# Gate and up projections run together, with a seven-product scheme on three of eight row pairs

## The chip, the cores and the metric

The kernel runs on one core of one Trainium2 chip. The core has a matrix engine (TensorE, in the profile PE for its matmuls and PEld for its weight loads), a vector engine (VectorE, DVE), an activation engine (ScalarE, ACT), GpSimd (POOL) and a queue engine (SyncE, SP) that here only issues DMAs. Matmul results land in PSUM, which has eight banks of 128 x 512 fp32; everything else lives in SBUF. The metric is the device time of one execution in microseconds, the median of several runs.

## What is computed

One hybrid decoder layer on 256 tokens of width 2048: a norm and an input projection, then attention and a state-space mixer side by side, an output projection with a residual, a SwiGLU feed-forward of inner width 5632, and a gated per-layer embedding. The change lies in the feed-forward:

```python
hf = rms_norm(x, g_ffn_norm[i])
x = x + (jax.nn.silu(hf @ w_gate[i]) * (hf @ w_up[i])) @ w_down[i]
```

`hf` is 256 x 2048, `w_gate` and `w_up` are 2048 x 5632, `w_down` is 5632 x 2048, all fp32.

## The kernel before

**Arithmetic.** Each fp32 operand is split into a high part (`hi`, type fp32r, made by an ACT copy) and a low part (`lo`, the fp32 value minus `hi`, made by a VectorE subtraction). A product is three matmuls, `hi*hi + hi*lo + lo*hi`, added up in one PSUM bank.

**Weights.** `Weights` cuts every weight matrix into chunks of 2 x 128 rows by up to 512 columns, in the order in which they are used. `load_to` issues a chunk's DMA on SP into one of `RAW = 5` raw buffers, `split_to` makes its high and low part in one of `PART = 3` buffers each, and `take(i)` asks for the splits up to chunk i+2 and the loads up to chunk i+7. The splits are written inside `high_priority(W_AHEAD)` with `W_AHEAD = 70`.

**Order of the instructions.** The program is written as one stream. A planner then orders each engine's queue: among the instructions that are ready it takes the one with the lowest rank, which is the place at which it was written, less 70 inside `high_priority(W_AHEAD)`, plus 25 for `gate_task` and plus 100 for `norm_task` (table `AHEAD`). Instructions inside such a block don't advance the rank of what follows. `Sched` runs small tasks (Python generators such as `norm_task` and `gate_task`) between the matmuls of a chunk. `S` hands out 39 SBUF slots of 4 KB per partition, `PP` four PSUM banks; the other four banks are the accumulators `acc`.

**Gate and up** (lines 1313 to 1346). For each of 11 blocks of 512 columns, `block` runs all 16 row tiles (k-tiles) of `w_gate`, then all 16 of `w_up`. Each run uses two accumulators, one per half of the tokens (t = 0, 1), so that a block alternates between two pairs of banks:

```python
for b in range(11):
    acc = block(blk["gu"][b][0], lhs_f, need_f if b == 0 else None)
    ...
        act(wsg[b % 2][:, t], acc[t], AF.Silu, scale=r_f[:, t:t + 1])
    acc = block(blk["gu"][b][1], lhs_f)
    for t in range(2):
        tt(wsg[b % 2][:, t], acc[t], wsg[b % 2][:, t])
    sched.add(gate_task(b), 0)
```

In `chunk` the last chunk of a run finishes token half 0 before half 1. `gate_task` transposes the gated block through a `PP` bank and splits it into `gh` and `gl`. `fh` and `fl` are the split, normed activations; `norm_task` makes them while the output projection runs, also through `PP` banks.

**Down** (lines 1349 to 1367) runs 44 row tiles for each of four column blocks, reading `gh` and `gl`. The parts of the per-layer embedding's input (`prh`, `prl`) are written behind its first block.

Of the kernel before, what the change touches and what calls it, by code (L numbers as in the profile page):

```python
# [11 lines left out]
F32 = mybir.dt.float32  # L12
# [129 lines left out]
class Weights:  # L142
# [4 lines left out]
    def __init__(self, tc, pool, sched):  # L147
        self.tc, nc = tc, tc.nc
        self.nc, self.pool, self.sched, self.chunks = nc, pool, sched, []
        self.raw, self.part, self.n_dma, self.n_split = {}, {}, 0, 0  # L150
        self.extra, self.native = {}, set()

    def block(self, w, k0, nk, c0, n):
        ids = []
# [21 lines left out]
    def split_to(self, i):  # L176
        while self.n_split <= min(i, len(self.chunks) - 1):
            self.load_to(self.n_split)
            n = self.chunks[self.n_split][3]
            raw = self.raw.pop(self.n_split)  # L180
            if self.n_split in self.native:
                self.part[self.n_split] = (raw, None, 0.0)
                self.n_split += 1
                continue
            hi = self.pool.tile([128, 2, n], F32R, tag="w_hi", bufs=self.PART, name="w_hi")
            lo = self.pool.tile([128, 2, n], F32R, tag="w_lo", bufs=self.PART, name="w_lo")
            with self.tc.high_priority(W_AHEAD):
                self.nc.scalar.activation(out=hi, in_=raw, func=AF.Copy)  # L188
                self.nc.vector.tensor_tensor(out=lo, in0=raw, in1=hi.bitcast(F32), op=ALU.subtract)  # L189
            s = self.sched  # L190
            s.act += 2 * n * 0.83e-3 + 0.19
            s.dve = max(s.dve + 2 * n * 1.05e-3 + 0.06, s.act)
            self.part[self.n_split] = (hi, lo, s.dve)
            self.n_split += 1

    def take(self, i):
        self.split_to(i + self.PART - 1)
# [7 lines left out]
def hybrid_layer_kernel(  # L205
# [35 lines left out]
    blk["glu"] = [W.block(w_glu, 0, 8, 512 * b, 512) for b in range(2)]  # L241
    blk["wos"] = [W.block(w_o, 8, 8, 512 * b, 512) for b in range(4)]
    blk["gu"] = []
    for b in range(11):
        blk["gu"].append((W.block(w_gate, 0, 16, 512 * b, 512), W.block(w_up, 0, 16, 512 * b, 512)))
    blk["down"] = [W.block(w_down, 0, 44, 512 * b, 512) for b in range(4)]
    blk["pp"] = [W.block(w_ple_proj, 0, 2, 512 * b, 512) for b in range(4)]
    blk["ple"] = [W.block(w_ple_gate, 0, 16, 512 * b, 512) for b in range(4)]
# [779 lines left out]
            sched.flags.add("oa")  # L1028


    def norm_task(xt, cb, ss, hi, lo, g0, flag):

        for t in range(2):
            pt = yield from pp_get("n")
            act(pt, xt(t, cb), AF.Square, accum_out=ss[:, cb, t:t + 1])
            PP.put(pt)
        for i0 in range(0, 4, 2):
            pt = yield from pp_get("n")
            for i in range(2):
                for t in range(2):  # L1040
                    transpose(quarter(pt, 2 * i + t), xt(t, cb)[:, (i0 + i) * 128:(i0 + i) * 128 + 128])
            yield None
            yield from splits(*((hi[cb][:, i0 + i], lo[cb][:, i0 + i], pt[:, i * 256:i * 256 + 256],
                                 gc[:, g0 + 4 * cb + i0 + i:g0 + 4 * cb + i0 + i + 1]) for i in range(2)))
            PP.put(pt)
        sched.flags.add(f"{flag}{cb}")
        yield 1
# [249 lines left out]

    fh = wait_n(4, [128, 4, 256], "fh", F32R)
    fl = wait_n(4, [128, 4, 256], "fl", F32R)
    lhs_s = tiles4(sh, sl, 8)  # L1300

    def need_s(k):
# [2 lines left out]
    for b in range(4):  # L1305
        acc = block(blk["wos"][b], lhs_s, need_s)
        sched.until("os")
        residual(acc, r_s, b)
        sched.add(norm_task(xv, b, ss_f, fh, fl, G_FFN, "hf"), 0)
    S.put(*sh, *sl)  # L1310


    lhs_f = tiles4(fh, fl)
    wsg = wait_n(2, [128, 2, 512], "wsg")
    gh, gl = [], []

    def gate_task(b):
        h = yield from S.get([128, 4, 256], "gh", F32R)
        l = yield from S.get([128, 4, 256], "gl", F32R)
        gh.append(h)  # L1320
        gl.append(l)
        f2 = lambda a: a.rearrange("p k n -> p (k n)")
        for i0 in range(0, 4, 2):
            pt = yield from pp_get("g")
            for i in range(2):
                for t in range(2):
                    transpose(quarter(pt, 2 * i + t), wsg[b % 2][:, t, (i0 + i) * 128:(i0 + i) * 128 + 128])
            yield None
            yield from splits((f2(h[:, i0:i0 + 2]), f2(l[:, i0:i0 + 2]), pt, None))
            PP.put(pt)  # L1330
        sched.flags.add(f"g{b}")

    def need_f(k):
        sched.until(f"hf{(k + 1) // 4}")

    for b in range(11):
        acc = block(blk["gu"][b][0], lhs_f, need_f if b == 0 else None)
        if b == 0:
            total_rstd(r_f, ss_f)
        for t in range(2):  # L1340
            act(wsg[b % 2][:, t], acc[t], AF.Silu, scale=r_f[:, t:t + 1])
        acc = block(blk["gu"][b][1], lhs_f)
        for t in range(2):
            tt(wsg[b % 2][:, t], acc[t], wsg[b % 2][:, t])
        sched.add(gate_task(b), 0)
    S.put(*fh, *fl)
    lhs_g = tiles4(gh, gl)

    def need_g(k):
        sched.until(f"g{k // 4}")  # L1350

    ph, pl = [], []
    for b in range(4):
# [122 lines left out]
```

## Time and profile before

| what | value |
| --- | --- |
| median of 3 runs | 1156.77 us (1155.93 to 1158.2) |
| the profiled execution: its time, its span | 1154.46 us, 1152.4 us |
| granted TensorE clock, mean | 0.999 |
| stretch of gate and up (316.1 to 804.6) | 488.5 us |
| stretch of down (804.6 to 1047.4) | 242.8 us |

The profile is one execution. Its span runs from the first to the last instruction; the execution's own time is 2.06 us longer. Rows give an engine, an operation, the tiles it writes and reads, a count, busy time and the mean of one in ns; "idle before" is the time in which the engine stood still just ahead of the group's instructions, with what ended it. Matmuls are pipelined: the time from one to the next is shorter than the duration shown.

### The profile page before, as it was taken

The numbers are of one execution on the slowest core, as the hardware profiler recorded it, in microseconds if no ns is written. First come the engines' busy times: TensorE is split into PE (matmuls) and PEld (weight loads), VectorE is DVE, ScalarE is ACT, GpSimd is POOL, SyncE is SP. The second block draws the span as 40 slices with busy tenths as digits, with TensorE's granted clock in tenths as the row PEclk, the third lists the DMA queues.
The fourth block names the chain that finished last, engine by engine and source line by source line (L and its number), as shares of the span: only waits on it lengthen the run. The fifth ranks groups of instructions, "written<-read, shape, count | busy, mean of one in ns | idle before, by whom it ended". The sixth has DMA issues, their size and how long they took to land.

```text
span 1152.4 us, 15432 instructions
## 1 busy us (share of the span) xinstructions
PE 1133.4 (98%) x5938; PEld 943.3 (82%) x5938; DVE 678.1 (59%) x949; ACT 573.7 (50%) x815; POOL 19.0 (2%) x40
## 2 busy tenths in 40 slices
PE   9998999999999999999999999999999999999998
PEld 6877877898888888888888888888888888888886
DVE  7989998657755455455454454455445454545554
ACT  7864984546554444444444444444444343436443
POOL 1000020000000000000000000000000000000000
PEclk9999999999999999999999999999999999999999
DMA  9996371355566666666666666666556556565662
GB/s 333 242 266 193 115 230 37 112 192 178 178 193 189 194 185 198 185 186 196 185 190 192 186 192 190 187 193 189 190 192 188 193 186 197 184 199 184 207 213 91
DMA packets 112185, 216.95 MB, mean 188 GB/s; under 512 B 8032, under 2 KB 12912, under 8 KB 112112
## 3 DMA queue, kind: packets, MB, share of 16 engines
q1 hardware_dynamic: 109808, 211.23, 60.5%
q0 software_dynamic: 2304, 4.74, 1.4%
q8 instruction: 46, 0.75, 0.3%
q14 instruction: 27, 0.22, 0.1%
HBM read 212.66 MB, written 3.28 MB: 187 GB/s over the span
## 4 chain that ended last, share of the span: by engine, by line
PE 88%; DVE 6%; ACT 2%; DMA 2%; issue 2%; POOL 0%; DVEq 0%; SPq 0%; ACTq 0%; POOLq 0%
PE acc L319 82%; DVE w_lo L189 1%; DMA e<-in_bE_dram 1%; PE pp_g L346 1%; PE pp_at L319 1%; DVE w L710 1%; PE pp_at L963 1%; PE pp_n L346 1%; PE pp_v L691 1%; ACT L315 1%; PE pp_y L745 1%; DVE w L303 1%; DVE wp L303 0%; ACT w_hi L188 0%; DMA rope<-in_ivf_dram 0%
## 5 line engine op out<-in xcount | busy, mean ns | idle before, releaser
L189 DVE TENSOR_TENSOR w_lo<-w_raw,w_hi 128x1024 fp32r<-128x1024 f32 (+2 forms) x382 | 462.3, 1211 | 435.4 <-ACT w_hi L188 435.0
L188 ACT ACTIVATE w_hi<-w_raw 128x1024 fp32r<-128x1024 f32 (+2 forms) x382 | 400.7, 1049 | 531.5 <-PE acc L319 520.0
L319 PE MATMUL acc<-w_hi,fh 128*128 128x512 f32 x704 | 274.9, 390 | 0.0
L319 PE MATMUL acc<-w_hi,fl 128*128 128x512 f32 x704 | 274.8, 390 | 0.0
L319 PE MATMUL acc<-w_lo,fh 128*128 128x512 f32 x704 | 274.0, 389 | 0.0
L319 PEld LDWEIGHTS acc<-w_hi,fl 128*128 128x128 f32 x704 | 132.2, 188 | 28.0
L319 PEld LDWEIGHTS acc<-w_lo,fh 128*128 128x128 f32 x704 | 132.2, 188 | 27.2
L319 PEld LDWEIGHTS acc<-w_hi,fh 128*128 128x128 f32 x704 | 132.2, 188 | 26.9
L319 PE MATMUL acc<-w_hi,gh 128*128 128x512 f32 x352 | 137.3, 390 | 0.0
L319 PE MATMUL acc<-w_hi,gl 128*128 128x512 f32 x352 | 137.1, 389 | 0.0
L319 PE MATMUL acc<-w_lo,gh 128*128 128x512 f32 x352 | 137.0, 389 | 0.0
L319 PEld LDWEIGHTS acc<-w_hi,gl 128*128 128x128 f32 x352 | 66.1, 188 | 13.9
L319 PEld LDWEIGHTS acc<-w_lo,gh 128*128 128x128 f32 x352 | 66.1, 188 | 13.6
L319 PEld LDWEIGHTS acc<-w_hi,gh 128*128 128x128 f32 x352 | 66.1, 188 | 13.4
L319 PE MATMUL acc<-w_hi,ph 128*128 128x512 f32 x128 | 49.8, 389 | 0.0
L319 PE MATMUL acc<-w_lo,ph 128*128 128x512 f32 x128 | 49.8, 389 | 0.0
L319 PE MATMUL acc<-w_hi,pl 128*128 128x512 f32 x128 | 49.8, 389 | 0.0
L319 PE MATMUL acc<-w_lo,hh 128*128 128x512 f32 (+1 forms) x120 | 45.2, 376 | 2.4 <-DVE w_lo L189 2.3
L319 PE MATMUL acc<-w_hi,hl 128*128 128x512 f32 (+1 forms) x120 | 44.3, 371 | 0.0
L319 PE MATMUL acc<-w_hi,hh 128*128 128x512 f32 (+1 forms) x120 | 44.3, 376 | 0.0
L319 PE MATMUL acc<-w_hi,o 128*128 128x512 f32 x128 | 41.6, 399 | 0.1
L319 PEld LDWEIGHTS acc<-w_lo,hh 128*128 128x128 f32 x120 | 22.5, 188 | 7.6 <-DVE w_lo L189 4.3
(275 smaller groups left out, 1181.7 us busy)
## 6 DMA issues: line engine op xcount, KB each, us to landing
w_raw<-in_w_gate_dram SPq DMA_DIRECT2D x88, 512.0 KB, 3.6
w_raw<-in_w_up_dram SPq DMA_DIRECT2D x88, 512.0 KB, 3.7
w_raw<-in_w_down_dram SPq DMA_DIRECT2D x88, 512.0 KB, 3.6
w_raw<-in_w_o_dram SPq DMA_DIRECT2D x32, 512.0 KB, 3.7
w_raw<-in_w_ple_gate_dram SPq DMA_DIRECT2D x32, 512.0 KB, 4.3
w_raw<-in_w_in_dram SPq DMA_DIRECT2D x24, 512.0 KB, 7.9
w_raw<-in_w_glu_dram SPq DMA_DIRECT2D x8, 512.0 KB, 3.6
w_raw<-in_w_uq_dram SPq DMA_DIRECT2D x8, 384.0 KB, 4.4
```

What stands on the lines that cost most here:

```text
L188: self.nc.scalar.activation(out=hi, in_=raw, func=AF.Copy)
L189: self.nc.vector.tensor_tensor(out=lo, in0=raw, in1=hi.bitcast(F32), op=ALU.subtract)
L303: V.tensor_tensor(out=o, in0=a, in1=b, op=op)
L315: A.activation(out=o, in_=i, func=f, **k)
L319: T.matmul(out=o, lhsT=a, rhs=b, start=start, stop=stop)
L346: T.transpose(out=o, in_=i, identity=ident if idt is None else idt)
L691: T.matmul(out=pv[p, r * 256 + i4 * 64:r * 256 + i4 * 64 + 64], lhsT=ee[r][p, i * 64:i * 64 + 64], rhs=um[p, i, :], start=True, stop=True, ...
L710: V.tensor_tensor_scan(out=w, data0=dc, data1=w, initial=0.0, op0=ALU.mult, op1=ALU.add)
L745: T.matmul(out=o, lhsT=a[p, i, :], rhs=f[p, i, :], start=False, stop=(r == 1), tile_position=(64 * s, 64 * s))
L963: T.matmul(out=o, lhsT=a, rhs=b_, start=False, stop=(i == 1), skip_group_check=True)
```

## The change

Row tiles are taken in eight pairs, and gate and up of a pair run together. With A the 2 x 2 block matrix of activations (token half by row tile of the pair) and W the 2 x 2 block matrix of weights (row tile of the pair by gate or up), a pair is a 2 x 2 block product. A plain pair computes its eight tile products. A mixed pair (pairs 2, 4 and 6; in block 0 only 4 and 6) uses the Winograd form of Strassen's scheme, with seven.

- `mix` makes, for a mixed pair, the five weight operands that the seven products need besides the gate chunk itself: four additions of 512 columns, and high and low parts of five 512-column tiles. It writes one set of tiles, `w_last`, `w_sum` and `w_mix`, used by every mixed pair in turn. The up chunk of a mixed pair is not split otherwise.
- `row_sums`, called from `norm_task`, makes the four sums of activation tiles for pairs 2, 4 and 6, once.
- `mixed_block` runs a block with all four accumulators. The four products that enter more than one result (P1, P5, P6, P7) collect over the mixed pairs of the block in the four `PP` banks; `shared` combines them in SBUF behind the last mixed pair, and the end of the block adds the accumulators.
- `gate_task` now only transposes and copies the gated block (`gr`); `need_g` splits it into `gh` and `gl` in the down stage, and frees its slot.

```diff
--- before.py
+++ after.py
@@ -149,6 +149,7 @@
         self.nc, self.pool, self.sched, self.chunks = nc, pool, sched, []
         self.raw, self.part, self.n_dma, self.n_split = {}, {}, 0, 0
         self.extra, self.native = {}, set()
+        self.mixed, self.kept, self.sums = set(), {}, None
 
     def block(self, w, k0, nk, c0, n):
         ids = []
@@ -178,6 +179,12 @@
             self.load_to(self.n_split)
             n = self.chunks[self.n_split][3]
             raw = self.raw.pop(self.n_split)
+            if self.n_split in self.mixed:
+                self.part[self.n_split] = self.mix(self.kept.pop(self.n_split - 1), raw)
+                self.n_split += 1
+                continue
+            if self.n_split + 1 in self.mixed:
+                self.kept[self.n_split] = raw
             if self.n_split in self.native:
                 self.part[self.n_split] = (raw, None, 0.0)
                 self.n_split += 1
@@ -192,6 +199,33 @@
             s.dve = max(s.dve + 2 * n * 1.05e-3 + 0.06, s.act)
             self.part[self.n_split] = (hi, lo, s.dve)
             self.n_split += 1
+
+    def mix(self, g, u):
+
+
+        V, A, s = self.nc.vector, self.nc.scalar, self.sched
+        last, raws, parts = self.sums
+
+        def add(o, a, b):
+            V.tensor_tensor(out=o, in0=a, in1=b, op=ALU.add)
+
+        def part(h, l, r):
+            A.activation(out=h, in_=r, func=AF.Copy)
+            V.tensor_tensor(out=l, in0=r, in1=h.bitcast(F32), op=ALU.subtract)
+
+        with self.tc.high_priority(W_AHEAD):
+            add(raws[0][:, 0], g[:, 0], u[:, 0])
+            add(raws[0][:, 1], u[:, 0], u[:, 1])
+            part(last[:, 0], last[:, 1], u[:, 1])
+            add(raws[1][:, 0], raws[0][:, 0], u[:, 1])
+            add(raws[1][:, 1], raws[1][:, 0], g[:, 1])
+            for r, (h, l) in zip(raws, parts):
+                part(h, l, r)
+        s.act += 5 * 512 * 0.83e-3 + 3 * 0.19
+        s.dve = max(s.dve + 9 * 512 * 1.05e-3 + 0.42, s.act)
+        (h0, l0), (h1, l1) = parts
+        return ((last[:, 0], last[:, 1]), (h0[:, 0], l0[:, 0]), (h0[:, 1], l0[:, 1]),
+                (h1[:, 0], l1[:, 0]), (h1[:, 1], l1[:, 1])), None, s.dve
 
     def take(self, i):
         self.split_to(i + self.PART - 1)
@@ -241,8 +275,14 @@
     blk["glu"] = [W.block(w_glu, 0, 8, 512 * b, 512) for b in range(2)]
     blk["wos"] = [W.block(w_o, 8, 8, 512 * b, 512) for b in range(4)]
     blk["gu"] = []
+    MIXED = (2, 4, 6)
     for b in range(11):
-        blk["gu"].append((W.block(w_gate, 0, 16, 512 * b, 512), W.block(w_up, 0, 16, 512 * b, 512)))
+        ids = []
+        for j in range(8):
+            ids.append((j, W.block(w_gate, 2 * j, 2, 512 * b, 512)[0], W.block(w_up, 2 * j, 2, 512 * b, 512)[0]))
+            if j in (MIXED[1:] if b == 0 else MIXED):
+                W.mixed.add(ids[-1][2])
+        blk["gu"].append(ids)
     blk["down"] = [W.block(w_down, 0, 44, 512 * b, 512) for b in range(4)]
     blk["pp"] = [W.block(w_ple_proj, 0, 2, 512 * b, 512) for b in range(4)]
     blk["ple"] = [W.block(w_ple_gate, 0, 16, 512 * b, 512) for b in range(4)]
@@ -1028,7 +1068,19 @@
             sched.flags.add("oa")
 
 
-    def norm_task(xt, cb, ss, hi, lo, g0, flag):
+    def row_sums(o, r):
+
+        tmp, hi, lo = o
+        a11, a21, a12, a22 = (r[:, 128 * i:128 * i + 128] for i in range(4))
+        s = [tmp[:, 128 * i:128 * i + 128] for i in range(4)]
+        tt(s[0], a22, a21, ALU.subtract)
+        tt(s[2], a11, a21, ALU.subtract)
+        tt(s[1], a11, s[0], ALU.add)
+        tt(s[3], a12, s[1], ALU.subtract)
+        act(hi, tmp, AF.Copy)
+        tt(lo, tmp, hi.bitcast(F32), ALU.subtract)
+
+    def norm_task(xt, cb, ss, hi, lo, g0, flag, mixed=None):
 
         for t in range(2):
             pt = yield from pp_get("n")
@@ -1042,6 +1094,15 @@
             yield None
             yield from splits(*((hi[cb][:, i0 + i], lo[cb][:, i0 + i], pt[:, i * 256:i * 256 + 256],
                                  gc[:, g0 + 4 * cb + i0 + i:g0 + 4 * cb + i0 + i + 1]) for i in range(2)))
+            if mixed is not None and 2 * cb + i0 // 2 in mixed:
+                k, o = 4 * cb + i0, mixed[2 * cb + i0 // 2]
+                w = yield from S.get([128, 2, 512], "rows")
+                for i in range(2):
+                    act(w[:, 0, 256 * i:256 * i + 256], pt[:, i * 256:i * 256 + 256], AF.Copy,
+                        scale=gc[:, g0 + k + i:g0 + k + i + 1])
+                yield None
+                row_sums((w[:, 1], o[:, 0], o[:, 1]), w[:, 0])
+                S.put(w)
             PP.put(pt)
         sched.flags.add(f"{flag}{cb}")
         yield 1
@@ -1297,6 +1358,7 @@
 
     fh = wait_n(4, [128, 4, 256], "fh", F32R)
     fl = wait_n(4, [128, 4, 256], "fl", F32R)
+    rows = {j: wait_get([128, 2, 512], "sum", F32R) for j in MIXED}
     lhs_s = tiles4(sh, sl, 8)
 
     def need_s(k):
@@ -1306,19 +1368,20 @@
         acc = block(blk["wos"][b], lhs_s, need_s)
         sched.until("os")
         residual(acc, r_s, b)
-        sched.add(norm_task(xv, b, ss_f, fh, fl, G_FFN, "hf"), 0)
+        sched.add(norm_task(xv, b, ss_f, fh, fl, G_FFN, "hf", rows), 0)
     S.put(*sh, *sl)
 
 
     lhs_f = tiles4(fh, fl)
     wsg = wait_n(2, [128, 2, 512], "wsg")
-    gh, gl = [], []
+    uc = wait_get([128, 2, 512], "uc")
+    W.sums = (wait_get([128, 2, 512], "w_last", F32R), wait_n(2, [128, 2, 512], "w_sum"),
+              [wait_n(2, [128, 2, 512], "w_mix", F32R) for _ in range(2)])
+    gr, gh, gl = [], [], []
 
     def gate_task(b):
-        h = yield from S.get([128, 4, 256], "gh", F32R)
-        l = yield from S.get([128, 4, 256], "gl", F32R)
-        gh.append(h)
-        gl.append(l)
+        h = yield from S.get([128, 4, 256], "g")
+        gr.append(h)
         f2 = lambda a: a.rearrange("p k n -> p (k n)")
         for i0 in range(0, 4, 2):
             pt = yield from pp_get("g")
@@ -1326,28 +1389,111 @@
                 for t in range(2):
                     transpose(quarter(pt, 2 * i + t), wsg[b % 2][:, t, (i0 + i) * 128:(i0 + i) * 128 + 128])
             yield None
-            yield from splits((f2(h[:, i0:i0 + 2]), f2(l[:, i0:i0 + 2]), pt, None))
+            act(f2(h[:, i0:i0 + 2]), pt, AF.Copy)
             PP.put(pt)
         sched.flags.add(f"g{b}")
-
-    def need_f(k):
-        sched.until(f"hf{(k + 1) // 4}")
+        yield 1
+
+    def products(o, a, w, first, last):
+        mm(o, a[0], w[0], first, False)
+        mm(o, a[0], w[1], False, False)
+        mm(o, a[1], w[0], False, last)
+        sched.pe += 3 * 0.227
+
+    def pair(j, cg, cu, acc, pq, lhs, rows, first, last):
+
+
+        k = W.chunks[cg][1]
+        wh, wl = W.take(cg)
+        G = [(wh[:, i], wl[:, i]) for i in range(2)]
+        if pq is None:
+            for c, cid in enumerate((cg, cu)):
+                if c:
+                    wh, wl = W.take(cid)
+                    G = [(wh[:, i], wl[:, i]) for i in range(2)]
+                for kk, t in ((0, 0), (1, 0), (0, 1), (1, 1)) if last else ((0, 0), (0, 1), (1, 0), (1, 1)):
+                    products(acc[2 * t + c], lhs(k + kk, t), G[kk], first and kk == 0, last and kk == 1)
+                    if t == 1:
+                        sched.step()
+            return
+        p1, p5, p6, p7, first, last = pq
+        r = [(rows[j][:, 0, 128 * i:128 * i + 128], rows[j][:, 1, 128 * i:128 * i + 128]) for i in range(4)]
+        products(p1, lhs(k, 0), G[0], first, last)
+        products(acc[0], lhs(k + 1, 0), G[1], False, False)
+        sched.step()
+        (w22, t1, t3, t2, t4), _ = W.take(cu)
+        products(acc[1], r[3], w22, False, False)
+        sched.step()
+        products(p5, r[0], t1, first, last)
+        products(p7, r[2], t3, first, last)
+        sched.step()
+        products(p6, r[1], t2, first, last)
+        products(acc[2], lhs(k + 1, 1), t4, False, False)
+        sched.step()
+
+    def shared(pq, a, b):
+
+        p1, p5, p6, p7 = pq[:4]
+        act(a[:, 0], p1, AF.Copy)
+        act(b[:, 1], p5, AF.Copy)
+        tt(b[:, 0], a[:, 0], p6, ALU.subtract)
+        tt(a[:, 1], b[:, 0], p7, ALU.add)
+        PP.put(*pq[:4])
+        tt(b[:, 0], b[:, 0], b[:, 1], ALU.add)
+        tt(b[:, 1], a[:, 1], b[:, 1], ALU.add)
+
...
+    def mixed_block(ids, lhs, rows, a, b, need):
+        acc = accs2() + accs2()
+        pq, left = None, sum(i[2] in W.mixed for i in ids)
+        n = left
+        for i, (j, cg, cu) in enumerate(ids):
+            need(j)
+            m = cu in W.mixed
+            if m and pq is None:
+                pq = [wait_pp("p") for _ in range(4)]
+            pair(j, cg, cu, acc, pq + [left == n, left == 1] if m else None, lhs, rows, i == 0, i == len(ids) - 1)
+            left -= m
+            if m and left == 0:
+                shared(pq, a, b)
+        return acc
+
+    def need_f(j):
+        sched.until(f"hf{j // 2}" if j < MIXED[1] else "hf3")
 
     for b in range(11):
-        acc = block(blk["gu"][b][0], lhs_f, need_f if b == 0 else None)
+        ws = wsg[b % 2]
+        acc = mixed_block(blk["gu"][b], lhs_f, rows, ws, uc, need_f)
         if b == 0:
             total_rstd(r_f, ss_f)
         for t in range(2):
-            act(wsg[b % 2][:, t], acc[t], AF.Silu, scale=r_f[:, t:t + 1])
-        acc = block(blk["gu"][b][1], lhs_f)
-        for t in range(2):
-            tt(wsg[b % 2][:, t], acc[t], wsg[b % 2][:, t])
+            tt(ws[:, t], ws[:, t], acc[2 * t], ALU.add)
+            act(ws[:, t], ws[:, t], AF.Silu, scale=r_f[:, t:t + 1])
+            tt(uc[:, t], acc[2 * t + 1], uc[:, t], ALU.subtract)
+            tt(ws[:, t], ws[:, t], uc[:, t])
         sched.add(gate_task(b), 0)
-    S.put(*fh, *fl)
+    S.put(*fh, *fl, *rows.values(), uc, W.sums[0], *W.sums[1], *W.sums[2][0], *W.sums[2][1])
     lhs_g = tiles4(gh, gl)
 
     def need_g(k):
-        sched.until(f"g{k // 4}")
+        while len(gh) <= min(k // 4 + 1, 10):
+            i = len(gh)
+            sched.until(f"g{i}")
+            gh.append(wait_get([128, 4, 256], "gh", F32R))
+            gl.append(wait_get([128, 4, 256], "gl", F32R))
+            split(gh[i], gl[i], gr[i])
+            S.put(gr[i])
 
     ph, pl = [], []
     for b in range(4):
```

More of the change, by code (lines that the diff above doesn't have):

```diff
@@ new lines, in shared, with wait_pp @@
+    def shared(pq, a, b):
[7 more added lines that the diff above has]
+        tt(b[:, 1], a[:, 1], b[:, 1], ALU.add)
+    def wait_pp(name):
+        n = 0
+        while True:
+            t = PP.try_get([128, 512], "pp_" + name)
+            if t is not None:
+                return t
+            sched.step()
+            sched.pe += 1.0
+            n += 1
+            if n > 2000:
+                raise RuntimeError("no bank")
```

## The prediction

> **What bounds the kernel now.** I read the page first (busy shares, slices, chain), then busy time by stage, then the groups kept apart by shape, and last the timeline at the end of a block. The page:
>
> ```profile
> span 1152.4 us, 15432 instructions
> PE 1133.4 (98%) x5938; PEld 943.3 (82%) x5938; DVE 678.1 (59%) x949; ACT 573.7 (50%) x815; POOL 19.0 (2%) x40
> PEclk9999999999999999999999999999999999999999
> ...
> PE 88%; DVE 6%; ACT 2%; DMA 2%; issue 2%; POOL 0%; DVEq 0%; SPq 0%; ACTq 0%; POOLq 0%
> ...
> w_raw<-in_w_up_dram SPq DMA_DIRECT2D x88, 512.0 KB, 3.7
> ```
>
> TensorE holds 98% of the span and 88% of the chain that ended last; the granted clock never drops. The stretches by stage (gate and up from 316.1, down from 804.6; columns are length, then busy us and instructions of PE, PEld, DVE, ACT, POOL, then clock, DMA share, GB/s):
>
> ```profile
> 272.00:316.00 44.00, 44.00 (x212) 36.83 (x211) 31.43 (x52) 25.42 (x41) 0.00 (x0) 1.00 0.59 180
> 316.10:804.60 488.50, 488.50 (x2200) 405.26 (x2199) 245.16 (x238) 214.73 (x228) 0.55 (x1) 1.00 0.66 190
> 804.60:1047.40 242.80, 242.80 (x1089) 201.41 (x1088) 118.94 (x112) 102.38 (x114) 0.00 (x0) 1.00 0.60 191
> ```
>
> In gate and up TensorE is busy for all of the 488.5 us, VectorE for half. So a matmul taken away is worth its whole pitch there, until another engine's work lands on the path. The pitch, and the rhythm of a weight chunk, from the timeline (start, length):
>
> ```profile
> 399.71 0.39 PE L319 MATMUL acc<-w_hi,fh 128*128 128x512 f32 x1
> 399.91 1.06 ACT L188 ACTIVATE w_hi<-w_raw 128x1024 fp32r<-128x1024 f32 x1 [1.66 <-PE acc L319]
> 401.00 1.23 DVE L189 TENSOR_TENSOR w_lo<-w_raw,w_hi 128x1024 fp32r<-128x1024 f32 x1 [1.50 <-ACT w_hi L188]
> 402.26 5.81 SPq L168 DMA_DIRECT2D w_raw<-in_w_gate_dram  x3
> 402.43 0.39 PE L319 MATMUL acc<-w_hi,fh 128*128 128x512 f32 x1
> ```
>
> 399.71 and 402.43 are twelve matmuls apart: 2.72/12 = 0.227 us each, 0.39 us from start to end. When a chunk's last reader ends (0.2 us after the next chunk begins), ACT copies the next high part into its buffer, VectorE makes the low part, and at 402.26 SP sends the next load into the raw slot just freed.
>
> **The change, part by part.**
>
> *Matmuls removed.* A plain pair of row tiles costs 2 k-tiles x 2 token halves x 2 (gate, up) x 3 = 24 matmuls; a mixed pair 7 x 3 = 21. Mixed pairs: 3 in ten blocks, 2 in block 0, so 32. 32 x 3 x 0.227 = **-21.8 us**. A block's PE time goes from 192 x 0.227 = 43.5 to 183 x 0.227 = 41.5 us, plus under 1 us of transposes in both.
>
> *VectorE in gate and up.* Rows for its prices:
>
> ```profile
> L189 DVE TENSOR_TENSOR w_lo<-w_raw,w_hi 128x1024 fp32r<-128x1024 f32 x366 | 448.4, 1225 | 435.4 <-ACT w_hi L188 435.0
> L303 DVE TENSOR_TENSOR wsg<-acc,wsg 128x512 f32<-128x512 f32 x22 | 14.1, 681 | 0.0
> L303 DVE TENSOR_TENSOR gl<-pp_g,gh 128x512 fp32r<-128x512 f32 x22 | 14.1, 681 | 0.0
> L315 ACT ACTIVATE gh<-pp_g 128x512 fp32r<-128x512 f32 x22 | 11.7, 584 | 0.0
> L303 DVE TENSOR_TENSOR po<-po,xs 128x512 f32<-128x512 f32 x6 | 4.1, 690 | 0.2
> L303 DVE TENSOR_TENSOR q_tok<-q_tok,rope 128x128 f32<-128x128 f32 x16 | 4.3, 289 | 0.0
> 359.30 1.23 DVE L189 TENSOR_TENSOR w_lo<-w_raw,w_hi 128x1024 fp32r<-128x1024 f32 x1 [1.49 <-ACT w_hi L188]
> 360.44 1.28 DVE L303 TENSOR_TENSOR wsg<-acc,wsg 128x512 f32<-128x512 f32 x2
> ```
>
> Back to back, a 1024-wide operation takes 360.44 - 359.30 = 1.14 us and a 512-wide one 1.28 - 0.68 = 0.60. Per block: 13 ordinary splits x 1.14 = 14.8; three mixes of five 512-wide and two 1024-wide operations, 3 x (3.0 + 2.28) = 15.8; `shared`, four, 2.4; the end of the block, six, 3.6. Sum 36.6 us; at full durations (1.225, 0.69) 40.2. Before, 245.16/11 = 22.3. So VectorE goes from half busy to 36.6 to 40.2 of 42.4 us: on average still under TensorE, with 2 to 6 us to spare. ACT adds three mixes of 0.58 + 2 x 1.06, two copies in `shared`, and drops the plain up splits: about 26 of 42.4 us, hidden.
>
> *Single buffers of the mix.* Each mix writes one set (`w_last`, `w_sum`, `w_mix`) that the mixed pair before still reads. Between two mixed pairs lies a plain one, 24 x 0.227 = 5.4 us, and the last-read tile (`w_mix[1]`) is needed 15 matmuls (3.4 us) into the next: 8.8 us for a copy and a subtraction of 2.3 us. Cost 0; without the plain pair it would not be.
>
> *The end of a block: the term I am least sure of.* Before, a block used two accumulator banks while the two others were evacuated. Now a block holds all four from its first to its last matmul, and the products P1, P5, P6, P7 hold the four others. The next block's matmuls therefore wait for evacuation. Take 0 as the issue of the block's last matmul. The last pair is plain, and its order ends gate half 0 at -4.1, gate half 1 at -2.7, up half 0 at -1.4, up half 1 at 0. The next block wants a first bank at 0, a second at 0.7 (1.4 if its order is shuffled), a third at 2.7, a fourth at 3.4. Evacuating takes one VectorE operation of 0.6 us a bank, 0.17 us after the matmul's start-to-start: alone, every bank would come free about 2 us early. Cost of this by itself: 0.
>
> But it isn't alone. `mix` is ranked 70 places ahead of where it is written (`high_priority(W_AHEAD)`), and its text for the next block's pair 2 stands 47 places behind the first evacuation (8 evacuation instructions, three loads, 36 matmuls), so it outranks evacuation by 23 places. That rank decides on readiness is seen here:
>
> ```profile
> L315 ACT ACTIVATE prh<-pr x1: 632/632/632, 788.7 to 788.7; 128x512 fp32r<-128x512 f32 x1
> L319 PE MATMUL acc<-w_hi,prh x16: 389/389/476, 1048.0 to 1059.1; 128*128 128x512 f32 x16
> ```
>
> `prh` is written behind the whole first down block and first read at 1048.0, yet it ran at 788.7, as soon as a slot of `fh` came free. So the mix for pair 2 runs as soon as its up chunk has landed. That chunk takes the raw slot that gate 0's split frees. Gate 0's buffer is free when pair 6 has used gate 6, at -8.8; plus 0.2, 1.06 and 1.23 with their waits, -6.3; plus 3.7 us to land, about -2.7. From there on 5.3 us of mix, two or three splits (1.14 each) and the evacuations want VectorE at once. Walked by hand with these prices: if the chunk lands before -2.6, only one bank is evacuated ahead of the mix, the next follow from 4.9 on, and the next block starts 2.9 us late in all (TensorE does 12 matmuls on the one bank meanwhile). If it lands between -2.5 and -0.3, two banks are free, TensorE has 5.4 us of work on them and the third comes at about 7.4: 2.0 us. If it lands later, three are free and nothing is lost. The stall is thus bounded by 0 and 2.9 us at each of ten boundaries; a gain is excluded, as TensorE already has no gap there. The trace has no block end with all banks in use, and the nearest row (3.7, a median, on an issue time of my walk) puts the landing 0.1 us off the first switch, with the queue ahead of it able to push it later. I take 1.0 us, between nothing and the 2.0 of the middle case, since any gap in the mix (it waits on ACT for three of its operations) lets a 0.6 us evacuation through: **+10 us**.
>
> On this the Trainium skill's page "Perfetto Trace Analysis", section "Optimizing Tensor Performance", says that independent matmul groups should rotate through different PSUM banks, so that evacuating one overlaps the next group's matmuls. The trace of before agrees as far as it goes: with that rotation TensorE is busy 488.50 of 488.50 us. By that rule the first rival below is what happens, and the sum would come out near no gain.
>
> *Row sums.* `row_sums` adds to `norm_task` three times four 128-wide operations and a 512-wide one, 3 x (4 x 0.289 + 0.69) = 5.5 us of VectorE, in and just behind the stretch before 316 where it is busy 31.43 of 44 us. The last is due for pair 6 of block 0, 30 us into the stage. Cost 0; uncovered, 1.8 us. The first block's third and fourth banks are those of the last residual:
>
> ```profile
> 316.03 1.40 DVE L311 SCALAR_TENSOR_TENSOR xs<-acc,r_s,xs 128x512 f32<-128x512 f32 x2
> ```
>
> It ends at 317.4; two free banks carry TensorE to 319. Cost 0.
>
> *Splits of the gated values.* In gate and up `gl` goes (2 x 0.68 us a block; already left out above). In down 11 x (1.06 ACT, 1.14 VectorE) = 12.5 us of VectorE fall into the first of four blocks (60.7 us, VectorE 49% busy): hidden. Only the first piece can hold TensorE: 0 if it is pulled ahead as `prh` was, about 2.5 if it follows the last evacuation. Three slots are free early, so I take **+1 us**. Bytes and loads are unchanged; SP's order too.
>
> *Sum.* -21.8 + 10 + 1 = -10.8 us. The profiled execution took 1154.46 us (span 1152.4 and 2.1 around it), 2.3 under the median of 1156.77. Against it: 1143.7; put to the median: **1146.0 us**.
>
> **The rivals.**
>
> *Mix ahead of evacuation (ends slower).* The stall is 2.0 to 2.9 us at ten boundaries: -21.8 + 20 to 29 + 1 gives +0 to +8, 1157 to 1165 us. For it: the ranks and the landing estimate above. Against it: it needs the landing before -0.3. It decides from 2.1 us a boundary on.
>
> *Evacuation all in time.* Stall 0 to 0.3: 1156.8 - 21.8 + 0 to 4 = 1135 to 1139. For it: the 2 us that every bank has when alone, and VectorE's 2 to 6 us of spare time a block. Against it: the crowd at -2.7 to 5.
>
> *VectorE becomes the bound; seven products then gain nothing.* It runs 13 + 21 + 4 + 6 = 44 operations a block, each behind ACT, a load or another operation. At 40.2 us, with 0.1 us lost before each, it needs 44.6 against 42.4: 2.2 us more in ten blocks, 1157; with 0.2 lost, 1179. Against it: back to back the trace shows overlap (0.60 for a 0.68), not loss.
>
> **How the numbers follow.** Forecast (stall 0.3 to 1.7, 1138 to 1153) 0.36; mix ahead 0.32, of which 0.12 lands within 0.2%; all in time 0.22; VectorE the bound 0.10. A difference under 0.2% (2.3 us) is about what a measurement of this kernel cannot tell from none. Faster 0.36 + 0.22 = 0.58; same 0.12; slower 0.20 + 0.10 = 0.30. The range takes in the all-in-time end and the mix-ahead end: 1134 to 1166; the likeliest case alone is 1138 to 1153.
>
> **What would show it.** Matmuls on `acc` and `pp_p` in gate and up: 2016 instead of 2112, pitch still 0.227. Gaps: waits of PE or its weight loads on VectorE's `ws`/`uc` operations, about ten, 1 us each; over 2 us each is the first rival, none the second. VectorE 37 to 40 us a block. PE gaps inside blocks, on `w_mix` or `w_lo`, would be the third. A wait of PE on `gl` at the start of down beyond 2.5 us would make the last term wrong, and a block pitch other than 42.4 us plus its stall would make the whole count wrong.

## The result, and the profile after

| kernel | median us (lowest to highest, runs) | ratio to before, 95% interval |
|---|---|---|
| before | 1157.49 (1155.93 to 1159.21, 4) | |
| changed | 1144.97 (1143.13 to 1147.23, 4) | 0.9892 [0.9867, 0.9918] |

The change makes the kernel 1.1% faster, by the medians 12.5 us. (The kernel before was run a fourth time, so its median is no longer 1156.77.) The profiled execution of the changed kernel took 1146.05 us, span 1144.1, against 1154.46 before: 8.4 us less. The page of the changed kernel:

```profile
span 1144.1 us, 15655 instructions
PE 1117.7 (98%) x5842; PEld 923.7 (81%) x5842; DVE 861.4 (75%) x1233; ACT 648.3 (57%) x921; POOL 19.0 (2%) x40
...
PE 78%; DVE 9%; DMA 5%; ACT 4%; issue 2%; POOL 0%; DVEq 0%; SPq 0%; ACTq 0%; POOLq 0%
...
w_raw<-in_w_up_dram SPq DMA_DIRECT2D x88, 512.0 KB, 4.6
```

96 matmuls fewer (5938 to 5842), as counted. In the chain that ended last TensorE gives up ten points (88% to 78%), and DMA and VectorE take six of them: something waits for loads now. An up chunk lands 4.6 us after its issue, not 3.7. The same stages as before (length, then busy us and instructions of PE, PEld, DVE, ACT, POOL, clock, DMA share, GB/s); gate and up is the first row, down the second:

```profile
317.50:796.40 478.90, 472.22 (x2106) 385.41 (x2105) 419.57 (x507) 282.15 (x323) 0.00 (x0) 1.00 0.63 194
796.40:1039.20 242.80, 242.80 (x1088) 201.20 (x1087) 126.73 (x120) 107.33 (x120) 0.55 (x1) 1.00 0.59 191
```

TensorE, without idle time before, is idle for 6.7 us of gate and up, and VectorE is busy for 419.57/478.9 = 88%, 38.1 us a block. What the two wait for in this stretch (total us, times, longest us):

```profile
DVE w_sum L210 <- DMA w_raw<-in_w_up_dram: 26.5, 21, 2.3
...
PEld acc L359 <- DVE uc L343: 12.4, 19, 1.7
PE acc L359 <- DVE uc L343: 5.8, 9, 1.3
```

VectorE waits 21 times for an up chunk, at the first additions of the mix. Ten of these waits, 9.4 us together, stand at the ends of blocks, the others inside them. TensorE waits for VectorE's evacuation into `uc`. The timeline of one block end ties the two together, VectorE first (start, length, operation, idle time before it and its releaser):

```profile
488.67 0.68 DVE L343 TENSOR_TENSOR wsg<-wsg,acc 128x512 f32<-128x512 f32 x1
489.27 0.69 DVE L343 TENSOR_TENSOR uc<-wsg,uc 128x512 f32<-128x512 f32 x1
490.62 1.29 DVE L210 TENSOR_TENSOR w_sum<-w_raw 128x512 f32<-128x512 f32 x2 [0.67 <-DMA w_raw<-in_w_up_dram]
491.84 1.22 DVE L196 TENSOR_TENSOR w_lo<-w_raw,w_hi 128x1024 fp32r<-128x1024 f32 x1
492.97 0.68 DVE L343 TENSOR_TENSOR uc<-acc,uc 128x512 f32<-128x512 f32 x1
...
492.93 0.39 PE L359 MATMUL acc<-w_hi,fl 128*128 128x512 f32 x1
493.71 0.50 PE L359 MATMUL acc<-w_hi,fh 128*128 128x512 f32 x1 [0.39 <-DVE uc L343]
494.04 0.39 PE L359 MATMUL acc<-w_lo,fh 128*128 128x512 f32 x1
```

By the count of its 183 matmuls the block ends with the issue at 492.25. One bank is evacuated at 488.67. Next in VectorE's queue stand the two additions of the next block's pair 2, and they wait for the up chunk: VectorE is idle from 489.96 to 490.62. Behind them stand a split and then the second evacuation, which ends at 493.65. TensorE issues three matmuls of the new block on the one free bank (492.47 to 492.93) and then stops for 493.71 - 492.93 - 0.227 = 0.55 us. At the other block ends the pattern is the same, with other sizes:

| idle of VectorE before the additions, us | 0.63 | 0.67 | 0.71 | 0.79 | 0.85 | 0.97 | 1.20 | 1.56 |
|---|---|---|---|---|---|---|---|---|
| TensorE's gap beyond its pitch, us | 0.52 | 0.55 | 0.60 | 0.68 | 0.74 | 0.86 | 1.09 | 1.44 |

The gap is VectorE's idle time less 0.11 us. (At the two ends left out it was 1.53 and 0.28, and 0.53 and 0.77. They fit too: at the first no split, 1.14 us, stands between the additions and the second evacuation, and at the other VectorE had been idle 0.36 us more a little earlier.) All ten gaps sum to 7.5 us.

The stage from its first matmul to the first of down took 488.75 us before and 478.86 after: -21.8 for the matmuls, +7.5 at the block ends, +4.4 in smaller losses: some 3.0 of it in single steps of 0.31 to 0.34 us from one matmul to the next (41 of them, 11 before), some 1.2 at a pitch of 0.23 to 0.24 us in places.

### The profile page after: what moved, and what is told of

Its sections match the earlier page's. It is cut to its first block, busy times and chain, and to the rows that moved or that the text cites. A ratio compares the mean times of both kernels' runs of the same rounds, so it can differ in the third digit from the quotient of the medians.

```text
span 1144.1 us, 15655 instructions
## 1 busy us (share of the span) xinstructions
PE 1117.7 (98%) x5842; PEld 923.7 (81%) x5842; DVE 861.4 (75%) x1233; ACT 648.3 (57%) x921; POOL 19.0 (2%) x40
## 4 chain that ended last, share of the span: by engine, by line
PE 78%; DVE 9%; DMA 5%; ACT 4%; issue 2%; POOL 0%; DVEq 0%; SPq 0%; ACTq 0%; POOLq 0%
PE acc L359 67%; PE pp_p L359 5%; DMA w_raw<-in_w_up_dram 4%; DVE w_lo L196 3%; ACT w_hi L195 2%; DMA e<-in_bE_dram 1%; PE pp_g L386 1%; PE pp_at L359 1%; DVE w L750 1%; PE pp_at L1003 1%; PE pp_n L386 1%; PE pp_v L731 1%; DVE w_sum L210 1%; ACT L355 1%; PE pp_y L785 1%
## 5 line engine op out<-in xcount | busy, mean ns | idle before, releaser
L359 PE MATMUL acc<-w_hi,fh 128*128 128x512 f32 x480 | 188.7, 396 | 5.9 <-DVE uc L343 5.8
L359 PE MATMUL acc<-w_lo,fh 128*128 128x512 f32 x480 | 188.1, 392 | 0.0
L359 PE MATMUL acc<-w_hi,fl 128*128 128x512 f32 x480 | 187.1, 390 | 0.0
L359 PEld LDWEIGHTS acc<-w_hi,fh 128*128 128x128 f32 x480 | 90.1, 188 | 30.9 <-DVE uc L343 12.4
L359 PEld LDWEIGHTS acc<-w_hi,fl 128*128 128x128 f32 x480 | 90.1, 188 | 18.8
L213 ACT ACTIVATE w_mix<-w_sum 128x1024 fp32r<-128x1024 f32 x64 | 67.9, 1062 | 50.3 <-DVE w_sum L210 38.5
L214 DVE TENSOR_TENSOR w_mix<-w_sum,w_mix 128x1024 fp32r<-128x1024 f32 x64 | 76.3, 1218 | 0.6
L359 PE MATMUL pp_p<-w_mix,sum 128*128 128x512 f32 x288 | 70.5, 389 | 0.0
L359 PEld LDWEIGHTS pp_p<-w_mix,sum 128*128 128x128 f32 x288 | 54.1, 188 | 11.2
L210 DVE TENSOR_TENSOR w_sum<-w_raw 128x512 f32<-128x512 f32 x64 | 42.2, 687 | 27.7 <-DMA w_raw<-in_w_up_dram 26.5
```

The costliest lines, as they stand in the source:

```text
L210: V.tensor_tensor(out=o, in0=a, in1=b, op=ALU.add)
L213: A.activation(out=h, in_=r, func=AF.Copy)
L214: V.tensor_tensor(out=l, in0=r, in1=h.bitcast(F32), op=ALU.subtract)
L359: T.matmul(out=o, lhsT=a, rhs=b, start=start, stop=stop)
```

## The experiments

Theory 1: VectorE stands still, in the order of its queue, at additions whose up chunk comes late, and the evacuations are behind it. Theory 2: it is the amount of mixing work that crowds the evacuations. Theory 3: it is the new block itself (gate and up together on four banks, the gated values split in down), whatever VectorE does.

Each kernel was also profiled; this table cuts those executions in three, at the first matmul of gate and up and the first of down (us):

| kernel | ahead of gate and up | gate and up | down to the end | span |
|---|---|---|---|---|
| before | 316.3 | 488.75 | 347.3 | 1152.4 |
| changed | 317.8 | 478.86 | 347.5 | 1144.1 |
| changed, run again | 319.4 | 478.63 | 347.4 | 1145.4 |
| later rank | 320.6 | 473.67 | 347.6 | 1141.8 |
| six load buffers | 324.7 | 469.08 | 347.7 | 1141.4 |
| two mixed pairs | 320.6 | 474.06 | 347.5 | 1142.1 |
| no mixed pairs | 321.1 | 488.91 | 347.5 | 1157.5 |
| a pair of spare buffers | 318.1 | 472.50 | 347.6 | 1138.1 |
| four mixed pairs | 322.2 | 476.74 | 353.2 | 1152.1 |
| sixth buffer in the ring | 318.8 | 469.40 | 347.3 | 1135.5 |

The first column moves by some us without an edit there (317.8 and 319.4 for one kernel), so the middle one is what the theories are read from. Most of that movement goes with the granted clock. In rows of 50 us ahead of the stage it falls below 1.00 between 50 and 100 us and between 150 and 200 us alone. What it lacks there, times 50 us, is an estimate of the time lost (us):

| | before | changed; spare buffers | changed again; sixth in the ring | later rank; two, no, four mixed pairs | six load buffers |
|---|---|---|---|---|---|
| lack of clock times 50 us | 0 | 1.5; 1.5 | 3.0; 3.0 | 5.0; 5.0, 5.0, 5.0 | 6.5 |
| first column beyond before's | 0 | 1.5; 1.8 | 3.1; 2.5 | 4.3; 4.3, 4.8, 5.9 | 8.4 |

**No mixed pairs.** Gate and up together, on four accumulators, with the gated values split in down; no products saved.

```diff
-    MIXED = (2, 4, 6)
+    MIXED = ()
 ...
-            tt(ws[:, t], ws[:, t], acc[2 * t], ALU.add)
-            act(ws[:, t], ws[:, t], AF.Silu, scale=r_f[:, t:t + 1])
-            tt(uc[:, t], acc[2 * t + 1], uc[:, t], ALU.subtract)
-            tt(ws[:, t], ws[:, t], uc[:, t])
+            act(ws[:, t], acc[2 * t], AF.Silu, scale=r_f[:, t:t + 1])
+            tt(ws[:, t], acc[2 * t + 1], ws[:, t])
```

> No pair is mixed: all eight products in every pair, no row sums, no mix; gate and up still run together on all four accumulators, and the gated values are still split in the down stage. Theories 1 and 2: no gap at the ends of blocks, since VectorE is half idle, so the time is that of the kernel before, 1156 to 1159. Theory 3 (holding all four banks costs by itself): 7 us or more above the kernel before.

Measured: 1156.01 us against 1157.6, ratio 0.9994 [0.9982, 1.0007] (it is worked out from the single runs, not from the two medians). Its gate and up:

```profile
321.14:810.05 488.91, 488.91 (x2201) 405.60 (x2200) 242.25 (x225) 224.34 (x237) 0.55 (x1) 1.00 0.61 190
```

TensorE is busy throughout, although all four accumulators of a block are held to its end. Theory 3 falls: running the two together and moving the split cost nothing that can be measured. (Here the `PP` banks are not held by products; with two mixed pairs, below, they are, and TensorE has no gap either.) With it falls a strict reading of the bank rotation that the prediction took from the Trainium skill's page "Perfetto Trace Analysis", section "Optimizing Tensor Performance": a block kept all four of its banks, and their evacuations were in time with no mix ahead of them at VectorE.

**Later rank.** The mix is ranked 20 places ahead of where it is written, not 70.

```diff
+MIX_AHEAD = 20
 ...
-        with self.tc.high_priority(W_AHEAD):
+        with self.tc.high_priority(MIX_AHEAD):
```

> Only the rank of the mix changes: 20 places ahead of where it is written, not 70, so that the evacuations of a block outrank it. Theory 1 (VectorE stands in its queue at the mix's first additions until the up chunk has landed, and two evacuations stand behind them): at most one addition still stands ahead, the next bank is free about 1.8 us earlier, and the ten gaps between blocks (7.5 us of TensorE in the changed kernel's profile) go: 1137 us, 1.7 to 1.9% under the kernel before. Theory 2 (VectorE simply has too much work around a block's end, whatever the load does): the evacuations go ahead here too, so the same 1137, but the mix is then late and TensorE waits on w_mix or w_last in pair 2 for some of it. Theory 3 (holding all four banks costs a gap whatever else runs): the gaps stay, 1145.

Measured: 1141.47 us, ratio 0.9865 [0.9845, 0.9885]; gate and up 473.67 us, 5.2 less than in the changed kernel. That is half of the gain expected. Its waits in that stretch, and VectorE at a block end:

```profile
DVE w_sum L211 <- DMA w_raw<-in_w_up_dram: 23.8, 21, 3.6
...
PEld pp_g L387 <- DVE wsg L344: 9.3, 14, 1.0
...
490.36 0.69 DVE L344 TENSOR_TENSOR uc<-wsg,uc 128x512 f32<-128x512 f32 x1
491.54 0.69 DVE L211 TENSOR_TENSOR w_sum<-w_raw 128x512 f32<-128x512 f32 x1 [0.49 <-DMA w_raw<-in_w_up_dram]
492.15 0.68 DVE L344 TENSOR_TENSOR wsg<-wsg,acc 128x512 f32<-128x512 f32 x1
492.74 1.22 DVE L197 TENSOR_TENSOR w_lo<-w_raw,w_hi 128x1024 fp32r<-128x1024 f32 x1
```

VectorE still waits for the up chunk at the same place, behind the first evacuation (7.2 us at the ten block ends). But only one addition is left there, so the second evacuation starts 0.61 us after the wait, not 2.35, and TensorE no longer waits for a bank. What waits instead are the transposes of the gated values (`pp_g`), whose input is the last operation of the block end; this costs some 5.6 us. So the wait and the work between two evacuations add up, and shortening either closes the gap.

**Six load buffers.** The raw ring gets a sixth buffer from the start of the kernel, and the slot pool gives one up.

```diff
-    RAW, PART = 5, 3
+    RAW, PART = 6, 3
 ...
-    S = Slots(big, [f"s{i}" for i in range(39)])
+    S = Slots(big, [f"s{i}" for i in range(38)])
```

> Six raw buffers in place of five (and 38 slots in place of 39), so the up chunk of a mixed pair is asked for one chunk earlier, about 2.7 us; the order of VectorE's queue at the end of a block is the same. Theory 1 (the wait for the load at the head of the queue): VectorE's idle time before the additions at a block's end (0.5 to 1.6 us each) goes, and the gaps of TensorE, 7.5 us in ten places, with it: 1137 us. Theory 2 (too much VectorE work around a block's end): the same work in the same order, so most of the gaps stay: 1143 to 1145. Theory 3 (four banks held): 1145.

Measured: 1146.4 us, ratio 0.9907 [0.9889, 0.9924], no better than the changed kernel in whole, where 1137 was expected; but gate and up took 469.08 us:

```profile
324.67:793.75 469.08, 469.08 (x2106) 386.29 (x2105) 420.35 (x507) 284.96 (x326) 0.00 (x0) 1.00 0.62 198
150.00:200.00 50.00, 43.27 (x340) 34.72 (x341) 43.66 (x123) 28.64 (x84) 6.30 (x12) 0.90 0.37 124
```

In the first row TensorE has no idle time, with the same amount of VectorE work (420.35 us busy), in the same order at nine of the ten block ends: theory 1, and theory 2 is hard to hold. The second row shows where the gain went: the stage starts 6.9 us later than in the changed kernel, behind a stretch in which TensorE is busy 43.27 of 50 us and its clock is 0.90. It isn't this one execution: all six show a mean clock of 0.990 to 0.993. Which of the two halves of the edit costs this there, the ring or the missing slot, was not tried apart.

**Two mixed pairs.** Pairs 4 and 6 only; 66 matmuls saved, 15.0 us, not 96.

```diff
-    MIXED = (2, 4, 6)
+    MIXED = (4, 6)
```

> Pairs 4 and 6 alone are mixed in every block: 22 mixed pairs, 66 matmuls less than before, not 96. The first mix of a block then comes two pairs (10.9 us) later and meets no evacuation. Theories 1 and 2: no gaps at the ends of blocks; 66 x 0.227 = 15.0 us saved and 0 to 2 given back: 1142.5 to 1145, the same as the changed kernel with a third fewer sevens. Theory 3 (four banks held): gaps of 0.5 to 1.4 us stay in ten places: 1150 to 1152.

Measured: 1144.55 us, ratio 0.9887 [0.9869, 0.9905], the changed kernel's time. Gate and up, and the wait at the additions:

```profile
320.58:794.64 474.06, 474.06 (x2136) 392.67 (x2135) 380.98 (x448) 268.64 (x305) 0.00 (x0) 1.00 0.61 195
...
DVE w_sum L210 <- DMA w_raw<-in_w_up_dram: 14.5, 19, 1.7
```

TensorE is busy for all of the stage: 488.75 - 15.0 = 473.8, so these two pairs bring all but 0.3 us of what they promise. The third pair, whose mix falls on the block end, saves 6.8 us more and costs more than that: 478.86. VectorE still waits 14.5 us for up chunks, 19 times, but in the middle of blocks, where the next evacuation is 15 us or more away, and TensorE loses nothing.

**A pair of spare buffers.** Up chunks of mixed pairs go into two slots that are free during gate and up, so they needn't wait for the ring.

```diff
+            if self.n_dma in self.mixed:
+                t = self.spare[self.n_spare % 2]
+                self.n_spare += 1
+            else:
+                t = self.pool.tile([128, 2, n], F32, tag="raw", bufs=self.RAW, name="w_raw")
 ...
+    W.spare = wait_n(2, [128, 2, 512], "w_spare")
```

> The changed kernel with two slots that stand free in the gate and up stage used as raw buffers for the up chunks of the mixed pairs; the five ordinary raw buffers and the 39 slots stay. Theory 1 (VectorE waits at the head of its queue for that chunk's load, with two evacuations behind): the chunk is there before it is wanted, the gaps go and the gate and up stage takes 469 to 470 us, not 479; nothing ahead of it changes, so the whole is 9 to 10 us under the changed kernel, 1134 to 1137. Theory 2 (too much VectorE work around a block's end): the work is the same, so half of the gaps or more stay: 1140 to 1145.

Measured: 1141.25 us against 1157.3, ratio 0.9862 [0.9847, 0.9877]; gate and up 472.50 us. About two thirds of the gain expected came, and the time alone would have gone to theory 2 by that forecast (1140 to 1145). The changed kernel itself, run again beside it,

> The changed kernel once more, on the chip on which the next two run: 1143 to 1147 us, a gate and up stage of 478 to 480 us with about 10 us of gaps at the ends of its blocks, each about as long as VectorE's idle time before the first addition of the next mix.

gave 1147.72 us, ratio 0.9918 [0.9903, 0.9933], and 7.3 us of gaps at its ten block ends, a little slower and with smaller gaps than expected. All 506 VectorE operations of its stage have the order that they had the first time, though the waits among them differ: the queue's order is fixed, and VectorE does not take what is ready. Of the 7.3 us the spare buffers leave 2.9. The waits of the kernel with spare buffers say why:

```profile
PEld acc L364 <- DVE uc L348: 5.5, 10, 0.7
DVE w_sum L215 <- DMA w_raw<-in_w_gate_dram: 5.3, 11, 1.2
```

No addition waits for an up chunk any more; eleven wait for the gate chunk, the other operand. Ten of these stand at the block ends, one addition now ahead of all four evacuations, and TensorE's gap is the idle time less 0.12 us at each of them. One late load was mended, and the next one behind it showed.

**Four mixed pairs.** Pairs 0, 2, 4 and 6 (4 and 6 in the first block), with the spare buffers; 42 x 3 = 126 matmuls saved, 28.6 us.

```diff
-    MIXED = (2, 4, 6)
+    MIXED = (0, 2, 4, 6)      # block 0: MIXED[2:]
```

> As the kernel with the two spare raw buffers, but pair 0 is mixed too (pairs 0, 2, 4, 6; in block 0 only 4 and 6): 30 + 10 + 2 = 42 mixed pairs, so 30 x 0.227 = 6.8 us less matmul time again, and 4.1 us more VectorE work in each of ten blocks: 40.7 us at back-to-back prices against 39.5 us of matmuls and 0.9 of transposes. If VectorE is the next bound: its busy share in gate and up reaches 95% or more, TensorE waits in the middle of blocks on w_lo, w_last or w_mix, and the time is no better than with three pairs, 1136 to 1142. If it is not: 1128 to 1130.

Measured: 1150.94 us, ratio 0.995 [0.9935, 0.9965]. Gate and up, and its waits:

```profile
322.15:798.89 476.74, 466.77 (x2075) 378.04 (x2074) 453.82 (x564) 296.87 (x344) 0.00 (x0) 1.00 0.63 192
...
PEld acc L364 <- DVE wsg L348: 14.2, 10, 1.4
PE acc L364 <- DVE wsg L348: 10.0, 10, 1.0
```

Saved 28.6, kept 12.0; the time lies above both ranges expected, and TensorE waits at the ends of blocks, not in their middle. VectorE is busy for 453.82/476.74 = 95%, and at each of the ten block ends TensorE has a gap of 1.13 to 1.16 us, with no load waited for and VectorE busy without a pause around it. This is theory 2, crowding: real, but beginning at four pairs, not at three. It is crowding in one place: a block has 180 matmuls, 40.9 us (the expectation's 39.5 is too low), and VectorE's 40.7 us would just fit beside them. Additions and splits stand ahead of the evacuations here too; whether a later rank would help was not tried. Another 5.8 us (353.2 for 347.4) go at the start of down, where TensorE waits for VectorE's last evacuations and for `gl`; whether the crowd does that or the two slots that the spare buffers hold was not tried apart.

**A sixth buffer in the ring, for gate and up alone.** From gate and up on, every sixth chunk goes to a free slot, so that the ring has six buffers there; as chunks are numbered, this is always a gate chunk. Ahead of it nothing changes.

```diff
+            if self.spare is not None and self.n_dma in self.sixth:
+                t = self.spare
+            else:
+                t = self.pool.tile([128, 2, n], F32, tag="raw", bufs=self.RAW, name="w_raw")
 ...
+        W.sixth.update(c for i in ids for c in i[1:] if c % 6 == 0)
 ...
+    W.spare = wait_get([128, 2, 512], "w_spare")
```

> The changed kernel with one free slot as a sixth raw buffer in the gate and up stage alone (every sixth chunk there goes into it); what lies ahead of that stage keeps its five buffers and its slots, and the order of VectorE's queue at the end of a block stays. Theory 1 (the wait for the up chunk's load at the head of VectorE's queue): gate and up takes 469 to 470 us, as with six buffers throughout, with no gap over 0.2 us at the ends of blocks, and the whole is 8 to 10 us under the changed kernel: 1136 to 1139. Theory 2 (too much VectorE work around a block's end): 1143 or more. If the loss seen ahead of gate and up with six buffers throughout was one of buffers and slots, it is absent here; if it was the clock in that run, it may come again.

Measured: 1137.61 us (1135.24 to 1139.41) against 1157.2, ratio 0.983 [0.981, 0.985]; the fastest here, ahead of the kernel before by 1.7% and ahead of the changed one, which ran at 0.9892 and 0.9918. Gate and up, its waits, and the same block end of VectorE:

```profile
318.76:788.16 469.40, 469.38 (x2105) 386.29 (x2104) 421.42 (x508) 285.18 (x326) 0.55 (x1) 1.00 0.64 197
...
ACT w_last L217 <- DMA w_raw<-in_w_up_dram: 29.2, 11, 3.0
...
PEld acc L364 <- DVE uc L348: 3.0, 10, 0.4
...
485.75 0.68 DVE L348 TENSOR_TENSOR wsg<-wsg,acc 128x512 f32<-128x512 f32 x1
486.35 0.68 DVE L348 TENSOR_TENSOR uc<-wsg,uc 128x512 f32<-128x512 f32 x1
486.95 1.29 DVE L214 TENSOR_TENSOR w_sum<-w_raw 128x512 f32<-128x512 f32 x2
488.18 1.23 DVE L200 TENSOR_TENSOR w_lo<-w_raw,w_hi 128x1024 fp32r<-128x1024 f32 x1
489.32 0.68 DVE L348 TENSOR_TENSOR uc<-acc,uc 128x512 f32<-128x512 f32 x1
```

At this and eight more of the ten block ends the operations of VectorE and their order are those of the changed kernel, line by line (elsewhere the order differs in places); only the idle time in front of the additions is gone, here 0.67 us, and with it TensorE's gap. That settles it for theory 1: same queue at the block ends, earlier data, 9.5 us less in the stage. The stage starts at 318.8 us, not at 324.7 as with six buffers from the start. The wait for loads itself is not gone: ACT now has 29.2 us of it, where nothing urgent stands behind it. Of the 21.8 us promised, 19.4 arrive. The 2.4 left are again single steps of 0.31 to 0.34 us (31, 11 before; 2.0 us) and a pitch of 0.23 to 0.24 us in places, less a little that the transposes gain. They are there with six buffers from the start too (2.1), which have no gaps, so they are not part of the stalls. Their cause was not found.

## Why the prediction was right

Forecast 1146.0, measured 1144.97: -10.8 us against -12.5 by the medians and -8.4 between the two profiled executions, whose clock ahead of gate and up differs. That the sum is so near is in part luck, as its terms show; each step by itself:

*Matmuls removed*: 96, at 0.227 us: as predicted.

*VectorE*: 38.1 us a block, inside 36.6 to 40.2. That it would not be the bound at three pairs was right, and the 2 to 6 us to spare are what four pairs used up. Two sums here are off without touching the forecast: at the prices named the upper figure is 40.5, not 40.2, and the rival with 0.2 us lost before each operation comes to 1201 us, not 1179.

*The end of a block* (+10): right in place and nearly in size, 7.5 us at the ten boundaries, 0.75 each for the 1.0 taken. The mechanism was half wrong. Right: the mix of pair 2 gets in front of the evacuations, and its up chunk lands near the block end. The walk put the landing at -2.7 with 3.7 us in flight; it was -1.6 in the block shown, with a median of 4.6 in flight. What failed is the sentence that a later landing costs less ("if it lands later, three are free and nothing is lost"). It supposes that VectorE takes whatever is ready, which the row of `prh` cannot show: that row fits an early place in a fixed queue as well. The traces show a fixed order: the additions stand behind the first evacuation and ahead of the second at this end and, with six buffers, at the same place, whether the chunk is there or not. So a late chunk is waited for, each 0.1 us of it beyond the first 0.11 is 0.1 us of TensorE, and an early one costs nothing. The walk's prices for an early landing, 2.0 to 2.9 us, failed too: it had 5.3 us of mix in one piece ahead of the third bank, while only two additions and a split (2.35 us) stand between two evacuations. The 1.0 us was a choice midway between nothing and 2.0, and that it was near the mark was luck: the reason is one that the walk did not contain. Had the landing been used as the walk has it, -1.6 would have given 2.0 us a boundary and a forecast of no gain.

*Mix ahead of evacuation*, the rival on the other side, had the right order of work and the wrong price; *all in time* is what a sixth buffer makes of it (1137.61, inside its 1135 to 1139).

*Row sums, first block's banks, single buffers of the mix* (0): nothing of them shows in the waits. Ahead of gate and up the changed kernel's profiled execution is 1.5 us later than before's, but its clock row for the stretch from 50 to 100 us reads 0.97 in place of 1.00, which by itself makes 1.5 us, and nothing that was added runs there; why the clock fell there is not shown.

*Splits of the gated values* (+1): 0. Down takes 242.80 us in both profiles, and TensorE is busy for all of it. With four pairs, where the cover is gone, 5.8 us are lost there.

*Not in the sum*: the 4.4 us of smaller losses. Together with 7.5 this is 11.9 us given back, where the sum had 11: a term 2.5 too high, one 1 too high and one missing made up for each other.

## What to carry to other kernels

Work that is moved ahead by rank keeps its place in an in-order queue: if its input is a load, ask not when the engine has time for it but what stands behind it while the load is late. The best mend here was then on the load's side, one more buffer, taken only in the stage that needs it. When a change saves less than its count, look at the seams of its loop first: here a third of the saving, 7.5 of 21.8 us, went into ten block ends and came back without touching the arithmetic.

## What the runs showed of the hardware

Gaps of TensorE can cost twice. At the start of down with four mixed pairs it had little to do for 3.7 us (busy 0.79), and the matmuls after it started 0.43 us apart, at a granted clock of 0.50 from 804.4 to 807.8, before they returned to 0.23 (columns as in the tables of stages above, then start and length):

```profile
800.30:804.00 3.70, 0.79 (x4) 0.20 (x2) 3.70 (x6) 0.72 (x1) 0.00 (x0) 1.00 0.59 180
804.40:807.00 2.60, 2.60 (x8) 2.03 (x7) 2.60 (x4) 1.06 (x1) 0.55 (x1) 0.50 0.16 58
...
804.77 0.63 PE L364 MATMUL acc<-w_hi,gh 128*128 128x512 f32 x1
805.19 0.63 PE L364 MATMUL acc<-w_lo,gh 128*128 128x512 f32 x1
...
808.66 0.40 PE L364 MATMUL acc<-w_hi,gl 128*128 128x512 f32 x1
```

By this the half clock cost, as an estimate, 1.7 of the 5.8 us that were lost there. The Trainium skill's page "TensorE: Matmul & The Clock Gate", section "What's actually happening", has the clock fall to half after an idle window of about 3.4 us and return after a busy one as long. This trace agrees in the size, 0.50, and in the 3.4 us until the return; the stretch ahead was not quite idle. The gaps at block ends of the changed kernel, 1.44 us at most, left the clock at 1.00 in the stage's row.

A first matmul after a stall runs 0.33 to 0.34 us to the next (493.71 to 494.04), not 0.227, at all ten block ends of the changed kernel, so such a stall costs 0.1 us more than its wait. It isn't the stall alone that does it: with the sixth buffer the same step of 0.34 us stands in nine blocks at a matmul that waited for nothing. What causes it was not found.
